# The last expert of a mixture-of-experts layer taken in the order of the others: its gate weights loaded ahead of the down weights of the expert before it, and its idle products removed

## The chip, the cores and the metric

The kernel runs on one core of a Trainium2 chip. The time is the device time of one execution in microseconds (us); several executions are timed, and their median counts. TensorE multiplies matrices, VectorE and ScalarE do elementwise work, SyncE (SP) issues the loads, which 16 transfer engines carry out. TensorE's clock has two levels, 1.2 and 2.4 GHz; the profile gives the granted clock as a share of the higher one.

## What is computed

One decoder layer for 256 tokens of width 1024: two attention branches, then 32 experts of which each token uses four, then a gated per-layer embedding (PLE). The change lies in the experts:

```python
def expert_block(args):
    xb, e = args
    gu = xb @ w_gate_up[e] + b_gate_up[e]
    g, u = gu[:, :D_EXPERT], gu[:, D_EXPERT:]
    g = jnp.minimum(g, SWIGLU_LIMIT)
    u = jnp.clip(u, -SWIGLU_LIMIT, SWIGLU_LIMIT)
    glu = g * jax.nn.sigmoid(SWIGLU_ALPHA * g)
    return ((u + 1.0) * glu) @ w_down[e] + b_down[e]
```

The rows of each expert are weighted and summed by token (`segment_sum`). Behind the experts comes `x + sigmoid(rmsnorm(x) @ w_ple_gate) * (p @ w_ple_proj)`.

## The kernel before

Every expert takes up to 64 tokens at once (an overflow loop handles more, and is not entered here). Its weights are float32: gate and up weights of 8 MiB in four tiles of 2 MiB, g0 to g3, and down weights of 4 MiB in two tiles, d0 and d1. Below, g31 stands for the gate and up weights of expert 31 or their products, d30 for the down weights of expert 30 or their products, and so on.

**Loads.** All weights stream through ten slots of 2 MiB in SBUF, in the order of the list `seq` (lines 138 to 147). `release` (line 150) is called when a tile has been used: it gives that slot to the next tile of the list, so a tile's load waits for the products that used the tile ten places earlier. SyncE issues the loads in that order at line 80; eight semaphore lanes are used in turn, so a load also waits until the load eight places earlier has landed. Only the last expert's tiles are loaded in two transfers of 1 MiB each. In the list, expert e's g tiles are followed by the d tiles of expert e-1; for the last expert (31) this is turned round: d30, then g31, then d31. Behind d31 come the two tiles of the PLE gate weights (w_ple, eight transfers of 0.5 MiB), then names that take a freed slot without a load: `low`, `hi`, `lo`, for the split halves of PLE operands.

**Products.** The loop over the experts is near line 945. `gate_up_k` (line 818) multiplies the gathered tokens xg with one k step of the gate and up weights, into the PSUM tiles g and u; a k step is four instructions of two passes each, an expert's eight k steps are 64 passes. `gate_up_bias` (line 812) adds the bias; `swiglu` (lines 822 to 828) is VectorE and ScalarE work; `hidden_T` (lines 834, 836) transposes the result on TensorE into PSUM and copies it on ScalarE to the tile ht. `down` runs 16 instructions of two passes (`down_k`, line 842) into the PSUM tile y and then `keep_y`: one half of y is copied to ys by ScalarE (line 846), the other by VectorE (line 847). Two experts share one ys; after each second expert `scatter` (line 852) adds both to the accumulators acc with eight passes. y, ht and ys have one buffer each.

In the loop, expert e's gate and up come first, then `down` of expert e-1, then the transposes of expert e: a down product fills the time of the swiglu. For the last expert `down` of 30 comes first; `keep_warm(WARM4, psum("y"))` issues 40 idle products (zeros, bfloat16, line 272) behind the bias. The instruction order on each engine is set by the tile framework's scheduler, which moved those 40 in among the gate products. Behind the loop come `down` of 31, ten idle products (WARM5), which the scheduler puts ahead of the transposes of 31, and the last scatter. Then acc is added to xs (line 999), xs is transposed (line 1004), and the PLE product runs with each operand split into a rounded part and a rest (w_hi, line 941, ScalarE; w_lo, line 942, VectorE; products at lines 251 to 253).

Of the kernel before, what the change touches and what calls it, by code (L numbers as in the profile page):

```python
# [33 lines left out]
NE = 32  # L34
# [20 lines left out]
FIRST_O = len(UNITS) - 8  # L55
LAST_THREE = 27

WARM0, WARM2, WARM3, WARM4, WARM5 = 30, 30, 8, 40, 10
AHEAD = 3

PLE_E, OVER_E = 14, 20
# [4 lines left out]
def hybrid_layer(ctx, tc, x, p, b_down, w_ple_gate, w_ple_proj, bgu3, xt, tabs, wpre, wgu, wdn, out):  # L66
# [59 lines left out]
    def bank(name):  # L126
        return ps_pool.tile([P, 512], F32, tag="ps", name=name)
# [12 lines left out]
    seq = []  # L140
    for e in range(NE):
        g = [(f"g{c}", e) for c in range(4)]
        d = [(f"d{c}", e - 1) for c in range(2) if e]
        seq += d + g if e == NE - 1 else g + d
        if e == PLE_E - 2:
            seq += [("aux", 0), ("pp", 0)]
        if e == OVER_E:
            seq += [("spare", 0), ("spare", 1)]
# [3 lines left out]
    def release(*slots):  # L152

        for i in slots:
            i = place.get(i, i)
            if sent[0] >= len(seq):
                return
            kind, e = seq[sent[0]]
            place[(kind, e)] = i
            t = v = slot(i, f"w_{kind}{e}")  # L160
            sent[0] += 1
            if kind[0] in "gd" and kind[1].isdigit():
                src = (wgu if kind[0] == "g" else wdn)[e, int(kind[1])]
                v = t.rearrange("p (k f) -> p k f", k=2 if kind[0] == "g" else 4)
                st = 2048 if e == NE - 1 else 4096
                for j in range(0, 4096, st):
                    load(t[:, j:j + st], src[:, j:j + st])
            elif kind == "aux":
                load(t[0:NE, 0:1024], b_down[0])
                load(t[:, 1024:1536].rearrange("p (t c) -> p t c", t=2), p[0, 0].rearrange("(t p) c -> t p c", p=P)  # L170
                     .rearrange("t p c -> p t c"))
                load(t[:, 2048:4096].rearrange("p (k f) -> p k f", k=2), w_ple_proj[0].rearrange("(k p) f -> p k f", p=P))
            elif kind == "ple":
                v = t.rearrange("p (k f) -> p k f", k=4)
                for k in range(4):
                    load(v[:, k], wpg[:, 4 * e + k])
            stream[(kind, e)] = v
# [90 lines left out]
    def keep_warm(n, b=None):  # L268

        b = bank("warm") if b is None else b  # L270
        for _ in range(n):
            T.matmul(b[:, 0:256], warm[:, 0:P], warm, start=True, stop=True)  # L272
# [441 lines left out]
    def work(tag, shape, bufs=1):  # L714
        return held[tag] if held else mo.tile(shape, F32, tag=tag, name=tag, bufs=bufs)
# [51 lines left out]
    def gather_pair(e):  # L767

        oh = work("oh", [P, 2, 2 * CAP])
        for tt in range(2):  # L770
            V.tensor_tensor(oh[:, tt].rearrange("p (j c) -> p j c", j=2), iota.rearrange("p (j c) -> p j c", j=2),
                            posm[:, tt, e:e + 2].unsqueeze(2).broadcast_to([P, 2, CAP]), op=ALU.is_equal)
        xg = work("xg", [P, 8, 2 * CAP])
        for half in range(2):
            b = psum("gu"[half])
            ks = slice(half * 4, half * 4 + 4)
            for k in range(4):
                for tt in range(2):
                    T.matmul(b[:, k * P:(k + 1) * P], h_perm[:, tt, (half * 4 + k) * P:(half * 4 + k + 1) * P],  # L779
                             oh[:, tt], start=(tt == 0), stop=(tt == 1))  # L780
            V.tensor_tensor(xg[:, ks], b.rearrange("p (k c) -> p k c", k=4),
                            gpk[:, 1, ks].unsqueeze(2).broadcast_to([P, 4, 2 * CAP]), op=ALU.mult)
        return xg, oh
# [3 lines left out]
    def weigh(ow, oh, wv_, odd):  # L787
        for tt in range(2):
            o = ow[:, tt].rearrange("p (g c) -> p g c", g=4)
            o = o[:, 1:3] if odd else o[:, 0:4:3]  # L790
            V.tensor_scalar(o, oh[:, tt:tt + 1].broadcast_to([P, 2, CAP]), wv_(tt), None, op0=ALU.mult)

    def weigh_pair(e, oh):
        ow = work("ow", [P, 2, S])
        for j in range(2):
            weigh(ow, oh[:, :, j * CAP:(j + 1) * CAP], wv_of(e + j), j)
        return ow
# [10 lines left out]
    def gate_up_bias(gu, se):  # L808
        for i in range(2):
            for half in range(2):  # L810
                w = bgu[:, i * 1024:(i + 1) * 1024].rearrange("e (q k) -> e q k", k=8)[:, :, half * 4:half * 4 + 4]
                T.matmul(gu[i][half * CAP:(half + 1) * CAP], se, w, start=False, stop=True)  # L812

    def gate_up_k(gu, xg, k, w):
        for i in range(2):
            for half in range(2):
                wv_ = w[:, i * 1024:(i + 1) * 1024].rearrange("p (q k) -> p q k", k=8)[:, :, half * 4:half * 4 + 4]
                T.matmul(gu[i][half * CAP:(half + 1) * CAP], xg[:, k], wv_, start=(k == 0), stop=False)  # L818

    def swiglu(gu):  # L820
        g = work("g", [P, 512])
        V.tensor_scalar_min(g, gu[0], 7.0)  # L822
        th = work("th", [P, 512])
        A.activation(th, g, AF.Tanh, scale=0.851)  # L824
        u = work("u", [P, 512])
        V.tensor_scalar(u, gu[1], 7.0, -7.0, op0=ALU.min, op1=ALU.max)
        V.scalar_tensor_tensor(u, in0=u, scalar=1.0, in1=g, op0=ALU.add, op1=ALU.mult)
        V.scalar_tensor_tensor(u, in0=th, scalar=1.0, in1=u, op0=ALU.add, op1=ALU.mult)
        return u

    def hidden_T(u):
        b = shared("hT")
        for j in range(4):
            T.transpose(b[:, j * P:(j + 1) * P], u.rearrange("p (q j) -> p q j", j=4)[:, :, j], ident)  # L834
        ht = work("ht", [P, 4, P])
        A.copy(ht, b.rearrange("p (j c) -> p j c", j=4))
        return ht

    def down_k(y, ht, f, w, odd):
        for dh in range(2):  # L840
            g = dh ^ odd
            T.matmul(y[g * CAP:(g + 1) * CAP], ht[:, f % 4, (f // 4) * CAP:(f // 4 + 1) * CAP],  # L842
                     w[:, dh * 512:(dh + 1) * 512], start=(f == 0), stop=(f == 7))

    def keep_y(ys, y, odd):
        A.copy(ys[0:CAP, odd], y[0:CAP])  # L846
        V.tensor_copy(ys[CAP:P, 1 - odd], y[CAP:P])  # L847
# [6 lines left out]
    def psum(tag):  # L854
        return held["ps_" + tag] if held else mps.tile([P, 512], F32, tag=tag, name=tag)
# [4 lines left out]
    def wv_of(e):  # L860
        return lambda tt: whalf[:, tt, e:e + 1]
# [65 lines left out]
    def down(e, ht, ys):  # L927
        y = psum("y")
        for f in range(8):
            down_k(y, ht, f, stream[(f"d{f // 4}", e)][:, f % 4], e % 2)  # L930
            if f % 4 == 3:
                release((f"d{f // 4}", e))
        keep_y(ys, y, e % 2)
# [10 lines left out]
    xg2, oh2 = gather_pair(0)  # L944
    weights()
    ow = weigh_pair(0, oh2)
    ht = None
    for e in range(NE):
        last, odd = e == NE - 1, e % 2
        if odd:  # L950
            ys = work("ys", [P, 2, 512])
        if last:
            down(e - 1, ht, ys)
        gu = [psum("g"), psum("u")]
        xg = xg2[:, :, odd * CAP:(odd + 1) * CAP]
        for k in range(8):
            gate_up_k(gu, xg, k, stream[(f"g{k // 2}", e)][:, k % 2])
            if k % 2:
                release((f"g{k // 2}", e))
        gate_up_bias(gu, id96[:, e:e + 1].broadcast_to([96, CAP]))  # L960
        u = swiglu(gu)
        if last:
            keep_warm(WARM4, psum("y"))
        else:
            if e:
                down(e - 1, ht, ys)
            if odd:
                xg2, oh2 = gather_pair(e + 1)
                ow = weigh_pair(e + 1, oh2)
        ht = hidden_T(u)  # L970
        if not odd:
            if e:
                scatter(ys, owT, first=(e == 2))
            owT = combine_T(ow)
        if e == OVER_E - 1:
            cnt = count()
        if e == OVER_E:
            overflow([stream[("spare", c)] for c in range(2)])
            release(("spare", 0), ("spare", 1))
        if e == PLE_E:  # L980
            aux = stream[("aux", 0)]
            pp = stream[("pp", 0)][:, 0:2048].rearrange("p (t c) -> p t c", t=2)
            down_bias()
            ple_projection()
            release(("aux", 0))
# [133 lines left out]
```

## Time and profile before

| | us |
|---|---|
| median of 3 timed runs | 1173.63 (1173.23 to 1173.77) |
| the profiled execution's own time | 1168.79 |
| its span, first to last instruction | 1167.0 |
| TensorE busy | 1083.0 (93%) |
| VectorE busy | 337.7 (29%) |
| ScalarE busy | 201.6 (17%) |
| transfer engines, share of the span taken by the weight queue q1 | 90.2% |
| mean granted clock of TensorE | 0.992 |

Busy times of TensorE are those of pipelined instructions with modelled ends: 16 passes of a down half lie 3.43 us long on the engine where the sum of their durations is far more. So durations of TensorE work are read from start to start. In the order of time a row has start, length, engine, line, operation, output<-inputs, shapes and count; the bracket gives the idle time ahead of it and what ended it. The chain of waits has start, length and what the end waited for there.

### The profile page before, as it was taken

How to read it: one execution, taken by the hardware profiler on the slowest of the kernel's cores; microseconds unless marked ns; L12 is line 12 of the kernel's file. 1: busy time of each engine (PE TensorE's matmuls, PEld its weight loads, DVE VectorE, ACT ScalarE, POOL GpSimd, SP SyncE). 2: the span in 40 equal slices, each digit the busy share in tenths (PEclk: the TensorE clock that was granted, in tenths of full speed). 3: DMA queues.
4: the chain of work that ended last, by engine and by line, in shares of the span. 5: the costliest groups of instructions: out<-in, count | busy, mean ns of one | idle time of the engine just before them, and what ended most of it. 6: DMA issues, size and time to landing. Idle time of an engine off the chain costs nothing. (4 is left out here: it accounts for less than half of the span.)

```text
span 1167.0 us, 13186 instructions
## 1 busy us (share of the span) xinstructions
PE 1083.0 (93%) x5486; PEld 529.2 (45%) x5486; DVE 337.7 (29%) x754; ACT 201.6 (17%) x375; POOL 78.5 (7%) x84
## 2 busy tenths in 40 slices
PE   8879999999999999998889999998899999998988
PEld 6668997543434343342333434333333333333336
DVE  7987686321111121121110111210111111111126
ACT  6557643210000000000001000000000000000024
POOL 6553320000000000000000000000000000000000
PEclk9999999999999999999999999999999999999999
DMA  9653568799999999999999999999899999999981
GB/s 368 223 177 108 200 209 323 288 430 430 431 430 431 430 429 430 431 431 411 431 431 431 431 430 430 431 430 426 349 430 430 431 430 431 431 430 430 425 352 37
DMA packets 39650, 440.19 MB, mean 377 GB/s; under 512 B 4384, under 2 KB 5152, under 8 KB 14144
## 3 DMA queue, kind: packets, MB, share of 16 engines
q1 hardware_dynamic: 39584, 439.27, 90.2%
q8 instruction: 46, 0.75, 0.2%
q14 instruction: 20, 0.16, 0.0%
HBM read 438.21 MB, written 1.05 MB: 376 GB/s over the span
## 5 line engine op out<-in xcount | busy, mean ns | idle before, releaser
L818 PE MATMUL g<-w_g,xg 128*64 128x512 f32 x1024 | 291.3, 599 | 26.7 <-DMA w_g<-in_wgu 22.2
L818 PE MATMUL u<-w_g,xg 128*64 128x512 f32 x1024 | 288.4, 595 | 0.0
L842 PE MATMUL y<-w_d,ht 128*64 128x512 f32 x1024 | 234.5, 596 | 12.5 <-DMA w_d<-in_wdn 11.7
L822 DVE TENSOR_SCALAR g<-g 128x512 f32<-128x512 f32 x32 | 22.1, 691 | 469.0 <-PE g L812 469.0
L818 PEld LDWEIGHTS g<-w_g,xg 128*64 128x64 f32 x1024 | 77.4, 137 | 169.1 <-issue 119.8
L818 PEld LDWEIGHTS u<-w_g,xg 128*64 128x64 f32 x1024 | 81.4, 137 | 145.5 <-issue 142.2
L842 PEld LDWEIGHTS y<-w_d,ht 128*64 128x64 f32 x1024 | 72.1, 136 | 137.2 <-issue 121.2
L824 ACT ACTIVATE th<-g 128x512 f32<-128x512 f32 x32 | 20.2, 630 | 487.9 <-DVE g L822 487.9
L847 DVE COPY ys<-y 64x512 f32<-64x512 f32 x32 | 22.2, 695 | 176.0 <-ACT ys L846 176.0
L852 PE MATMUL acc<-ys,owT 128*128 128x512 f32 x128 | 59.2, 605 | 9.5 <-ACT ys L846 9.5
L846 ACT COPY ys<-y 64x512 f32<-64x512 f32 x32 | 18.5, 578 | 262.0 <-PE y L842 262.0
L852 PEld LDWEIGHTS acc<-ys,owT 128*128 128x128 f32 x128 | 23.0, 189 | 46.5 <-ACT ys L846 21.8
L779 PE MATMUL g<-oh,h_perm 128*128 128x128 f32 x256 | 33.1, 282 | 6.8 <-DVE g L822 5.6
L210 ACT CAST fr<-raw_x 128x1024 fp32r<-128x1024 f32 (+1 forms) x33 | 33.9, 1033 | 22.5 <-PE proj L253 5.9
L779 PEld LDWEIGHTS g<-oh,h_perm 128*128 128x128 f32 x256 | 29.9, 191 | 16.9 <-DVE g L822 10.6
L214 POOL TENSOR_TENSOR fr<-raw_x,fr 128x384 fp32r<-128x384 f32 (+1 forms) x25 | 34.3, 1375 | 44.8 <-ACT fr L210 37.7
L214 DVE TENSOR_TENSOR fr<-raw_x,fr 128x640 fp32r<-128x640 f32 (+2 forms) x33 | 33.0, 999 | 6.2 <-ACT fr L210 6.0
L779 PEld LDWEIGHTS u<-oh,h_perm 128*128 128x128 f32 x256 | 29.8, 192 | 8.1 <-issue 8.1
L779 PE MATMUL u<-oh,h_perm 128*128 128x128 f32 x256 | 32.2, 279 | 0.0
L252 PE MATMUL proj<-fr,fr 128*128 128x512 f32 (+1 forms) x64 | 25.8, 403 | 6.9 <-DVE fr L214 6.2
L251 PE MATMUL gate<-fr,fr 128*128 128x256 f32 x104 | 31.2, 300 | 0.0
L253 PE MATMUL gate<-fr,fr 128*128 128x256 f32 x104 | 30.1, 290 | 0.0
(317 smaller groups left out, 1133.4 us busy)
## 6 DMA issues: line engine op xcount, KB each, us to landing
w_g<-in_wgu SPq DMA_DIRECT2D x124, 2048.0 KB, 31.1
w_d<-in_wdn SPq DMA_DIRECT2D x62, 2048.0 KB, 33.5
raw_x<-in_wpre SPq DMA_DIRECT2D x38, 512.0 KB, 4.2
w_g<-in_wgu SPq DMA_DIRECT2D x8, 1024.0 KB, 28.1
raw<-in_wpre SPq DMA_DIRECT2D x8, 512.0 KB, 6.6
w_d<-in_wdn SPq DMA_DIRECT2D x4, 1024.0 KB, 19.7
w_ple<-in_w_ple_gate SPq DMA_DIRECT2D x8, 512.0 KB, 14.5
raw<-in_wpre SPq DMA_DIRECT2D x4, 416.0 KB, 7.2
```

The lines of the kernel that those rows point to most:

```text
L210: A.copy(hi, src)
L214: e.tensor_tensor(lo[:, a:b], src[:, a:b], hi[:, a:b], op=ALU.subtract)
L251: T.matmul(o, lh, rh, start=first, stop=False)
L252: T.matmul(o, lh, rl, start=False, stop=False)
L253: T.matmul(o, ll, rh, start=False, stop=last)
L779: T.matmul(b[:, k * P:(k + 1) * P], h_perm[:, tt, (half * 4 + k) * P:(half * 4 + k + 1) * P], oh[:, tt], start=(tt == 0), stop=(tt == 1))
L818: T.matmul(gu[i][half * CAP:(half + 1) * CAP], xg[:, k], wv_, start=(k == 0), stop=False)
L822: V.tensor_scalar_min(g, gu[0], 7.0)
L824: A.activation(th, g, AF.Tanh, scale=0.851)
L842: T.matmul(y[g * CAP:(g + 1) * CAP], ht[:, f % 4, (f // 4) * CAP:(f // 4 + 1) * CAP], w[:, dh * 512:(dh + 1) * 512], start=(f == 0), stop= ...
L847: V.tensor_copy(ys[CAP:P, 1 - odd], y[CAP:P])
L852: T.matmul(acc[tt][dh], owT[:, dh, tok(tt)], ys[:, dh], start=first, stop=last)
```

## The change

It takes away three special cases of the last expert: the turned order in the list of loads, `down` of expert 30 ahead of the gate products of 31, and the 40 idle products. `down` of 30 now stands behind swiglu of 31, as for every other expert.

```diff
-WARM0, WARM2, WARM3, WARM4, WARM5 = 30, 30, 8, 40, 10
+WARM0, WARM2, WARM3, WARM5 = 30, 30, 8, 10
@@
         d = [(f"d{c}", e - 1) for c in range(2) if e]
-        seq += d + g if e == NE - 1 else g + d
+        seq += g + d
@@
         last, odd = e == NE - 1, e % 2
         if odd:
             ys = work("ys", [P, 2, 512])
-        if last:
-            down(e - 1, ht, ys)
         gu = [psum("g"), psum("u")]
@@
         u = swiglu(gu)
-        if last:
-            keep_warm(WARM4, psum("y"))
-        else:
-            if e:
-                down(e - 1, ht, ys)
-            if odd:
-                xg2, oh2 = gather_pair(e + 1)
-                ow = weigh_pair(e + 1, oh2)
+        if e:
+            down(e - 1, ht, ys)
+        if odd and not last:
+            xg2, oh2 = gather_pair(e + 1)
+            ow = weigh_pair(e + 1, oh2)
         ht = hidden_T(u)
```

How instructions move is shown at three places; the semaphores that an instruction waits for stand in brackets (DMAHW is a lane of the loads, Activation is ScalarE, DVE VectorE). In w_g031 the digits are tile 0 of expert 31.

SyncE, the loads of the last two experts, before:

```order
L80 DMA w_d129_5729<-in_wdn 128x4096 [waits DMAHW6_49,PE_49]
L80 DMA w_d030_5739<-in_wdn 128x4096 [waits DMAHW7_49,PE_49]
L80 DMA w_d130_5762<-in_wdn 128x4096 [waits DMAHW0_49,PE_49]
L80 DMA w_g031_5772<-in_wgu 128x2048 [waits DMAHW1_49,PE_49]
L80 DMA w_g031_5772<-in_wgu 128x2048 [waits DMAHW2_49]
```

and after:

```order
L80 DMA w_d129_5729<-in_wdn 128x4096 [waits DMAHW6_49,PE_49]
L80 DMA w_g031_5739<-in_wgu 128x2048 [waits DMAHW7_49,PE_49]
...
L80 DMA w_g331_5825<-in_wgu 128x2048 [waits DMAHW6_49]
L80 DMA w_d030_5836<-in_wdn 128x4096 [waits DMAHW7_49,PE_49]
L80 DMA w_d130_5846<-in_wdn 128x4096 [waits DMAHW0_49,PE_49]
L80 DMA w_d031_5856<-in_wdn 128x2048 [waits DMAHW1_49,PE_49]
```

The two loads of d30 moved behind the eight of g31; d31 and the w_ple loads behind it keep their places and lanes.

TensorE, from the second down half of expert 29 on, after (before, the sixteen instructions of d30 stood behind the transposes of ow at line 804, with g31 and the 40 idle products behind them):

```order
L842 MATMUL y_5871<-w_d129_5729,ht_5813 64x512 x7
L818 MATMUL g_5917<-w_g031_5739,xg_5782 64x512 [waits DMAHW7_49,PE_49]
L852 MATMUL acc_2250<-ys_5698,owT_5691 128x512 [waits Activation_49]
L852 MATMUL acc_2249<-ys_5698,owT_5691 128x512 [waits DVE_49]
L852 MATMUL acc_2251<-ys_5698,owT_5691 128x512
L852 MATMUL acc_2252<-ys_5698,owT_5691 128x512
L804 MATMUL owT_5910<-cst_62,ow_5803 128x128 [waits PE_49,Activation_49]
L804 MATMUL owT_5910<-cst_62,ow_5803 128x128 x3
L818 MATMUL g_5917<-w_g031_5739,xg_5782 64x512
```

One instruction (two passes) of g31 moved ahead of the scatter, and g31 follows owT directly. Further down, TensorE's end of the experts, after:

```order
L834 MATMUL hT_5992<-cst_62,u_5967 128x128 x3
L842 MATMUL y_5971<-w_d030_5836,ht_5903 64x512 [waits DMAHW7_49]
L842 MATMUL y_5971<-w_d030_5836,ht_5903 64x512 x7
L842 MATMUL y_5971<-w_d130_5846,ht_5903 64x512 [waits DMAHW0_49]
L842 MATMUL y_5971<-w_d130_5846,ht_5903 64x512 x7
L842 MATMUL y_5999<-w_d031_5856,ht_5997 64x512 [waits DMAHW1_49,DVE_49,Activation_49]
...
L852 MATMUL acc_2250<-ys_5916,owT_5909 128x512 [waits Activation_49]
L852 MATMUL acc_2252<-ys_5916,owT_5909 128x512
L852 MATMUL acc_2249<-ys_5916,owT_5909 128x512 [waits DVE_49]
```

d30 now lies between the transposes and d31, and the first product of d31 waits for VectorE and ScalarE, where before it waited for ScalarE alone.

ScalarE there, after:

```order
L824 ACTIVATE th_5965<-g_5963 128x512 [waits DVE_49,Activation_49]
L846 COPY ys_5916<-y_5971 64x512 [waits PE_49,Activation_49]
L836 COPY ht_5997<-hT_5992 128x512 [waits Activation_49]
L941 ACTIVATE w_hi0_5949<-w_ple0_5891,cst_62 128x1024 [waits DMAHW4_49,DMAHW5_49,DMAHW3_49,DMAHW6_49,DMAHW2_49,DMAHW7_49,DMAHW1_49,DMAHW0_49]
L846 COPY ys_5916<-y_5999 64x512 [waits PE_49]
```

The copy of expert 30's ys moved from ahead of line 824 to between it and the copy of ht; the first w_hi (line 941) stands ahead of the last copy of ys, and did before.

## Rows read from the trace of the kernel before

**Rows 1.** The page, transfer queues: packets, MB, share of 16 engines.

```profile
q1 hardware_dynamic: 39584, 439.27, 90.2%
```

**Rows 2.** Chain of waits from 1030 us on: start, length, what.

```profile
1046.23 39.91 DMA w_d<-in_wdn
1086.18 3.68 PE y L842 x16
```

**Rows 3.** TensorE in order of time, two windows (1056 and 1086 us on).

```profile
1058.34 0.64 PE L834 MATMUL hT<-cst,u 128*128 128x128 f32 x4
1058.91 3.65 PE L842 MATMUL y<-w_d,ht 128*64 128x512 f32 x16
...
1086.18 3.65 PE L842 MATMUL y<-w_d,ht 128*64 128x512 f32 x16 [0.42 <-DMA w_d<-in_wdn]
1090.52 3.70 PE L852 MATMUL acc<-ys,owT 128*128 128x512 f32 x8 [0.68 <-ACT ys L846]
...
1094.58 7.09 PE L842 MATMUL y<-w_d,ht 128*64 128x512 f32 x32
1101.50 1.03 PE L818 MATMUL g<-w_g,xg 128*64 128x512 f32 x4
...
1103.32 1.16 PE L272 MATMUL y<-warm 128*128 128x256 bf16 x9
...
1115.48 1.03 PE L818 MATMUL g<-w_g,xg 128*64 128x512 f32 x4
...
1119.77 1.03 PE L818 MATMUL u<-w_g,xg 128*64 128x512 f32 x4
1120.63 0.40 PE L812 MATMUL g<-bgu,id 96*64 96x512 bf16 x2
...
1123.93 0.75 PE L834 MATMUL hT<-cst,u 128*128 128x128 f32 x4 [0.87 <-DVE u L828]
1125.41 7.09 PE L842 MATMUL y<-w_d,ht 128*64 128x512 f32 x32 [0.73 <-ACT ht L836]
1133.17 1.12 PE L852 MATMUL acc<-ys,owT 128*128 128x512 f32 x2 [0.68 <-ACT ys L846]
```

**Rows 4.** SyncE's loads in order of time; then the w_ple tile's issues.

```profile
1098.37 7.79 SPq L80 DMA_DIRECT2D w_d<-in_wdn  x4
1108.36 17.38 SPq L80 DMA_DIRECT2D w_ple<-in_w_ple_gate  x8
...
L80 SPq DMA_DIRECT2D w_ple<-in_w_ple_gate x8: 327/328/328, 1108.4 to 1125.4; - x8
```

**Rows 5.** ScalarE (ACT), then VectorE (DVE), in order of time.

```profile
1089.88 0.58 ACT L846 COPY ys<-y 64x512 f32<-64x512 f32 x1 [8.05 <-PE y L842]
...
1126.92 1.15 ACT L941 ACTIVATE w_hi<-w_ple,cst 128x1024 fp32r<-128x1024 f32 x1 [1.57 <-DMA w_ple<-in_w_ple_gate]
1132.54 0.58 ACT L846 COPY ys<-y 64x512 f32<-64x512 f32 x1 [4.47 <-PE y L842]
1133.02 3.22 ACT L941 ACTIVATE w_hi<-w_ple,cst 128x1024 fp32r<-128x1024 f32 x3
...
1090.49 0.69 DVE L847 COPY ys<-y 64x512 f32<-64x512 f32 x1 [7.27 <-ACT ys L846]
1128.10 1.28 DVE L942 SCALAR_TENSOR_TENSOR w_lo<-w_ple,cst,w_hi 128x1024 fp32r<-128x1024 f32 x1 [4.23 <-ACT w_hi L941]
```

**Rows 6.** TensorE at 800.68; stretches: length, busy times, granted clock, transfer share, GB/s.

```profile
800.68 1.59 PE L818 MATMUL g<-w_g,xg 128*64 128x512 f32 x4 [3.96 <-PEq L898]
...
801.00:804.60 3.60, 3.60 (x12) 1.25 (x10) 0.00 (x0) 0.00 (x0) 0.00 (x0) 0.53 1.02 423
804.60:810.00 5.40, 5.40 (x28) 2.19 (x26) 0.00 (x0) 0.00 (x0) 0.00 (x0) 1.00 1.02 434
1120.60:1125.41 4.81, 2.65 (x21) 1.65 (x17) 2.67 (x4) 1.22 (x2) 0.00 (x0) 1.00 1.01 420
```

## The prediction

> **What bounds the kernel now.** I read the page first, then the chain of waits, then the order of time of each engine behind the point where the chain leaves the transfers. The weight queue q1 fills 90.2% of the transfer engines over the whole span [rows 1], and up to 1086.18 us the chain consists of landings: its last link there is a 39.91 us transfer of down weights [rows 2]. At 1086.18 TensorE starts the second half of expert 29's down product, released by that landing; behind it TensorE's rows name copies and VectorE as releasers, and no transfer [rows 3]. So the change, which touches nothing ahead of that point, has to be judged in the last 80 us, where the chain runs over TensorE: scatter, both down halves of expert 30 (1094.58), gate and up of expert 31 (1101.50 to 1120.63), bias, transposes (1123.93), down of 31 (1125.41), then the copies and the scatter.
>
> Two prices come from there. Six entries of gate/up, 1115.48 to 1120.63, take 5.15 us: 0.858 us an entry of 4 passes, 0.2146 us a pass, 13.73 us for an expert's 64 passes, 3.43 us for a down half of 16 [rows 3]. The stretch 1101.50 to 1120.63 is 19.13 us long, so the 40 idle products in it cost 5.40 us, on the path and not beside it.
>
> **The stream after the change.** The same bytes go out in the same place: 4 MiB of d30 ahead of 8 MiB of gate weights before, behind them now. Each load waits on the lane of the load eight earlier (the brackets of the listed order), so an issue time shows that one's landing: the first load of d31 went out at 1098.37, when the first 1 MiB piece of g31 had landed, the first ple load at 1108.36, when its fifth piece had [rows 4]. Counted from d29's landing at about 1086.15, that is 5 MiB in 12.2 us and 9 MiB in 22.2 us: 2.45 us per MiB, an estimate from these rows. The last of the eight ple loads went out at 1125.4, when the last piece of d31 had landed [rows 4]; 16 MiB by 2.453 from 1086.15 gives the same. So after the change: g31's eight pieces land at 1088.6, 1091.1 ... 1105.8; d30's halves at 1110.7 and 1115.6; d31's four pieces at 1118.0, 1120.5, 1122.9 and 1125.4, as before; the first ple piece unchanged. These loads also wait for their slots. The first ple load is a close one: it goes out when g31's seventh piece has landed, at about 1103.3, and its slot is freed by the first half of d29, which lies ahead of 1086.18: 17 us of cover. So I cost the queue at nothing; if that cover were gone, a late load would eat the slack of step 6 first and then count in full.
>
> **TensorE after the change, step by step.**
> 1. At 1089.61 (1086.18 plus 3.43) it has 0.91 us to wait for the copy of ys, since the scatter starts at 1090.52 [rows 3, 5]. Two passes of g31 now stand ahead of the scatter and fit there: 0.43 us gained. Their piece landed at 1088.6.
> 2. Scatter and owT end at 1094.58 as before. Then 62 passes of g31: 13.31 us, to 1107.89. Each of the eight k steps starts after its piece; the closest is the last, 1106.2 against 1105.8. The 5.40 us of idle products are gone.
> 3. Bias, clamps, ten idle products and transposes follow at the old distance, 1120.63 to 1123.93: transposes at 1111.19. The next down half follows transposes that nothing holds up after 0.57 us (1058.34 to 1058.91) [rows 3]: d30 starts at 1111.76, its weights landed at 1110.7. Before, d31 had to wait 1.48 us there for the copy of ht: 0.91 us gained.
> 4. The second half of d30 is wanted at 1115.19 and lands at 1115.6: 0.4 us lost. End 1119.06.
> 5. A new wait: y and ht have one buffer each. ys of expert 30 must leave y, and ht of 31 can be written only when d30 has read the old ht; both copies stand in that order on ScalarE, and VectorE copies its half of ys after ScalarE's. The same pattern after 1089.61 takes 0.27 us to ScalarE's copy, 0.58 for it, then 0.69 on VectorE, to 1091.18 [rows 5], and about 0.05 to the waiting product (there the scatter starts 0.06 us after ScalarE's copy ends). So d31 starts 1.62 us after 1119.06, at 1120.68: 1.62 us lost; no product is left to fill it. Queued behind it are d31 and the tail.
> 6. d31's 32 passes take 6.87 us, to 1127.55; its pieces are wanted at 1120.68, 1122.4, 1124.1 and 1125.83 and land at 1118.0, 1120.5, 1122.9 and 1125.4. Slack at the last: 0.4 us. Before, the end was 1132.28. Sum for TensorE: -5.40 - 0.43 - 0.91 + 0.4 + 1.62 = -4.7 us.
> 7. The first w_hi stands ahead of the last ys copy on ScalarE. In the trace it runs from 1126.92, released by its transfer, for 1.15 us, and is hidden by d31 [rows 5]. The cover shrinks: the copy could start 0.26 us after d31, as before (1132.28 to 1132.54), at 1127.81; it starts when the w_hi has ended, at 1128.0 to 1128.1. 0.2 us lost. The first w_lo (1128.10, 1.28 us) also delays VectorE's copy, to 1130.0, but only the third scatter product needs that one, 1.7 us after the first.
>
> By the Trainium skill (TensorE: Matmul & The Clock Gate, section on the array's architectural detail, queue depths) ScalarE and VectorE are strictly first in, first out, which speaks against the change in step 7: work that is ready waits behind the w_hi. No row of the trace shows a ready copy held. By the rule the sum is -4.5; if the copy could pass the w_hi it would be -4.7.
>
> The scatter starts 0.63 us after the start of that copy, as before: about 4.5 us earlier (1133.17 to 1128.6). The tail's VectorE and ScalarE work hangs on it, and the ple pieces are there in time: w_hi 2 to 4 follow each other every 1.07 us (3.22 for three [rows 5]), from 1128.5 on; at the stream's rate a 0.5 MiB piece comes every 1.2 us, the second at 1127.9 and the fourth at 1130.3, wanted at 1130.6. By the same rate the eighth lands by 1135.3, before the second four w_hi, which stand behind the transposes, begin. So the tail moves whole. 1168.79 - 4.5 = 1164.3 us for a profiled execution; that execution was 4.84 us under the median of the runs, 1173.63, so for the median **1169.1 us**.
>
> Bounds: the gain can't pass 5.2 us (last piece of d31 at 1125.4, its four passes and more 1.72 us, end 1127.1). From below: step 5 bounded by twice its row, step 4 by a piece that comes a whole piece (2.45 us) later, give a gain of 4.5 - 1.6 - 2.1 = 0.8 us if both happened; either alone leaves 2.4 to 2.9.
>
> **Rivals.**
> - *A clock dip, then a smaller gain.* Without idle products TensorE stands 1.62 us (step 5) and 1.1 us (ahead of the scatter) right behind d30 and d31. Against it: between 1120.60 and 1125.41 it worked only 2.65 us of 4.81, in pieces, and the granted clock stayed 1.00. For it: after one wait of 3.96 us the clock of the following 3.6 us averaged 0.53, half of 2.4 GHz [rows 6]. One such dip loses 3.6 x 0.47 = 1.7 us: gain 2.8, 1170.8 us. Chance 0.10. The Trainium skill (the same page, HAM oscillation) warns of exactly this, a TensorE that waits between bursts and starts each again slow; the trace agrees at that one wait, and doesn't at the shorter ones between 1120.60 and 1125.41.
> - *Slower: the clock at half through the whole end.* d30, d31, scatter and the ple products are now packed between short waits; if each wait brought a dip, the loss is half the time at 1.2 GHz. It decides at 9 us of half clock (4.5 us lost). Half clock from 1111.8 to 1127.5 doubles 64 passes: 13.7 us lost, 1178.3 us. Behind the wait of 3.96 us the clock was back at 1.00 from 804.60 on [rows 6], so a dip didn't last. Chance 0.03.
> - *The stream is the new bound, little gain.* If the pieces of d30 or d31 come late, TensorE waits for them with all 64 down passes still to do, where before 32 of them were done early. A stream 3.5 us late at d30's second half gives a loss of 3.9 in place of 0.4, 1172.6 us: no change that can be told. For it: all slack is 0.4 us. Against: same bytes, same lanes, 2.45 us per MiB on both checks. Chance 0.06, and 0.05 more for a lag of 1 to 2 us, 1170.1 to 1171.1.
> - *The change doesn't do what it says*, and the loads keep their order: the listed order shows them moved. No change in time; chance 0.01.
>
> **Numbers.** Forecast 1169.1 us, chance 0.75. Range 1167.6 (a gain of 6.0: the bound of 5.2 and 0.8 for two medians of runs that spread by 0.54 us) to 1171.2 (dip, or the short lag). About 0.2%, 2.35 us here, is what a measurement can tell from no change: faster by more 0.90, within it 0.07, slower 0.03.
>
> **What would show it.** In the new profile: TensorE's gate/up of 31 unbroken from 1094.6 to 1107.9 with no transfer named; d30 at about 1111.8; an idle of 1.6 us before d31 put down to a ys or ht copy; scatter near 1128.6 right behind a ScalarE queue of w_hi and ys; granted clock 1.00 throughout. Wrong would be: transfer waits above 0.5 us inside g31, a clock under 1.00 after 1111, or the tail's first ple product waiting on w_hi or w_lo.

## The result and the profile after

The changed kernel took 1166.79 us (median of 4 runs, 1165.23 to 1167.72), the kernel before beside it 1173.7 us (4 runs, 1173.23 to 1174.87): 0.9942 of the time, 95% interval 0.9928 to 0.9956, a gain of 6.9 us. The forecast was 1169.1 us in a range of 1167.6 to 1171.2, a gain of 4.5 us: the direction is right, the time lies 0.8 us below the range.

| | before | after |
|---|---|---|
| the profiled execution's own time, us | 1168.79 | 1165.23 |
| its span, us | 1167.0 | 1163.5 |
| q1's share of the span | 90.2% | 90.7% |
| second half of d29 to the last scatter, us | 46.99 | 42.62 |
| last scatter to the end of the span, us | 33.83 | 33.9 |

The fourth row is the length of the stretch that the change touches, from the last product that a transfer releases to the scatter: 1086.18 to 1133.17 in [rows 3], and 1086.98 to 1129.60 here. It is 4.37 us shorter. The chain of waits shows the same layout: the last landing, then TensorE to the end of the experts (start, length, what ended there).

```profile
1046.94 40.00 DMA w_d<-in_wdn
1086.98 3.65 PE y L842 x16
...
1121.84 7.10 PE y L842 x32
1128.97 0.59 ACT ys L846
1129.60 2.00 PE acc L852 x4
```

TensorE of the changed kernel in order of time, columns as in [rows 3]:

```profile
1086.98 3.65 PE L842 MATMUL y<-w_d,ht 128*64 128x512 f32 x16 [0.43 <-DMA w_d<-in_wdn]
1090.47 1.02 PE L818 MATMUL g<-w_g,xg 128*64 128x512 f32 x2
1091.42 3.70 PE L852 MATMUL acc<-ys,owT 128*128 128x512 f32 x8
...
1095.49 0.64 PE L818 MATMUL g<-w_g,xg 128*64 128x512 f32 x1
...
1108.46 0.40 PE L812 MATMUL g<-bgu,id 96*64 96x512 bf16 x1
1108.69 0.39 PE L812 MATMUL u<-bgu,id 96*64 96x512 bf16 x1
1108.85 0.59 PE L818 MATMUL u<-w_g,xg 128*64 128x512 f32 x1
1109.28 0.39 PE L812 MATMUL g<-bgu,id 96*64 96x512 bf16 x1
1109.51 0.39 PE L812 MATMUL u<-bgu,id 96*64 96x512 bf16 x1
1110.45 1.25 PE L272 MATMUL g<-warm 128*128 128x256 bf16 x10 [0.56 <-DVE g L822]
1112.57 0.75 PE L834 MATMUL hT<-cst,u 128*128 128x128 f32 x4 [0.87 <-DVE u L828]
1113.25 7.09 PE L842 MATMUL y<-w_d,ht 128*64 128x512 f32 x32
1121.84 7.09 PE L842 MATMUL y<-w_d,ht 128*64 128x512 f32 x32 [1.51 <-ACT ht L836]
1129.60 3.70 PE L852 MATMUL acc<-ys,owT 128*128 128x512 f32 x8 [0.67 <-ACT ys L846]
```

Two passes of g31 stand ahead of the scatter; g31 runs unbroken; d30 has taken the place of d31 behind the transposes, without the 0.73 us wait for ht; d31 has the new wait of 1.51 us. No row behind 1086.98 names a transfer. ScalarE's rows for the end, then VectorE's copy of the other half of expert 30's ys:

```profile
1120.43 0.58 ACT L846 COPY ys<-y 64x512 f32<-64x512 f32 x1 [9.31 <-PE y L842]
1120.92 0.58 ACT L836 COPY ht<-hT 128x512 f32<-128x512 f32 x1
1127.63 1.15 ACT L941 ACTIVATE w_hi<-w_ple,cst 128x1024 fp32r<-128x1024 f32 x1 [6.13 <-DMA w_ple<-in_w_ple_gate]
1128.97 0.58 ACT L846 COPY ys<-y 64x512 f32<-64x512 f32 x1 [0.19 <-PE y L842]
...
1121.05 0.69 DVE L847 COPY ys<-y 64x512 f32<-64x512 f32 x1 [8.53 <-ACT ys L846]
```

The first w_hi ends at 1128.78; the copy behind it waits 0.19 us more, for TensorE, so w_hi held nothing. SyncE's rows give the stream (start and length of a group of issues):

```profile
1089.47 12.50 SPq L80 DMA_DIRECT2D w_d<-in_wdn  x6
1104.13 22.36 SPq L80 DMA_DIRECT2D w_ple<-in_w_ple_gate  x8
```

The first w_ple load goes out at 1104.13 (forecast: 1103.3, and this execution stands 0.80 us later), the last at 1126.49 (1104.13 and 22.36; forecast 1125.4, and 0.80). The stream ran as worked out, to 0.3 us.

So one question is left: the profile shows 4.4 us, the first runs 6.9.

### The profile page after: what moved, and what is told of

It is laid out like the page before. It is cut to its first block, busy times and chain, and to the rows that moved or that the text cites. A ratio compares the mean times of both kernels' runs of the same rounds, so it can differ in the third digit from the quotient of the medians.

```text
span 1163.5 us, 13110 instructions
## 1 busy us (share of the span) xinstructions
PE 1076.0 (92%) x5446; PEld 525.8 (45%) x5446; DVE 337.9 (29%) x754; ACT 201.4 (17%) x375; POOL 78.2 (7%) x84
## 3 DMA queue, kind: packets, MB, share of 16 engines
q1 hardware_dynamic: 39584, 439.27, 90.7%
HBM read 438.21 MB, written 1.05 MB: 378 GB/s over the span
## 5 line engine op out<-in xcount | busy, mean ns | idle before, releaser
L818 PE MATMUL g<-w_g,xg 128*64 128x512 f32 x1024 | 295.4, 597 | 28.3 <-DMA w_g<-in_wgu 24.3
L818 PE MATMUL u<-w_g,xg 128*64 128x512 f32 x1024 | 292.5, 593 | 0.0
L210 ACT CAST fr<-raw_x 128x1024 fp32r<-128x1024 f32 (+1 forms) x33 | 33.9, 1033 | 21.8 <-PE proj L253 5.6
```

The lines of the kernel that those rows point to most:

```text
L210: A.copy(hi, src)
```

## The experiments

All distances run from the start of d29's second half. "Interval" ends at the last scatter, "end" at the end of the span. The runs come in groups ("calls" in the expectations), each on one chip; "beside" means the runs of the kernel before in the same group. The ratio is that of the kernel to the runs beside it, with its 95% interval; it is not exactly the ratio of the two medians.

**The two kernels again (b2, a2).** No edit.

> The kernel before, once more. The interval read in each profile here is the one from the start of d29's second half on TensorE to the start of the last scatter; it was 46.99 us before and 42.62 us after the change, 4.37 us less, where the medians of the runs differ by 6.9 us. Theory A: the change is worth its interval, 4.4 us; the other 2.5 us are chance between executions, lost far ahead of d29 (the granted clock was 0.96 in 600 to 640 us and in 780 to 820 us of the one profile of before, and 1.00 in that of after). Then this profile shows 47.0 us (within 0.3) whatever its span, and a span longer than 1167 comes with more stretches under 1.00 ahead of 1080 us. Theory B: the profile of before was an untypical execution, and in its timed runs the end itself is longer, by a clock under 1.00 or a transfer wait behind d29. Then a profile with a span near 1172 us shows an interval near 49.4 us.

> The changed kernel once more. Theory A: interval 42.6 us (within 0.3), time 4 to 5 us under the kernel before when enough runs of both are taken (ratio 0.996). Theory B: ratio 0.994 again (7 us), with this interval unchanged and that of before longer.

b2: 1171.89 us (12 runs, 1166.87 to 1175.67) and beside it 1171.58 (33 runs). a2: 1167.75 us (10 runs), ratio 0.9964 [0.9951, 0.9978], 3.8 us. The first base, 1173.2 to 1174.9, lay high in a spread of 8.8 us. The interval of a2 is 42.62 us, as in the first profile. That of b2 is 48.69 (from 1086.82), neither theory's figure, 47.0 or 49.4:

```profile
1124.57 0.75 PE L834 MATMUL hT<-cst,u 128*128 128x128 f32 x4 [0.87 <-DVE u L828]
1126.04 8.78 PE L842 MATMUL y<-w_d,ht 128*64 128x512 f32 x32 [0.73 <-ACT ht L836]
1135.51 3.70 PE L852 MATMUL acc<-ys,owT 128*128 128x512 f32 x8 [0.68 <-ACT ys L846]
```

d31 takes 8.78 us where it took 7.09 in [rows 3]: 1.69 us more, all of the difference. The windows around it (length, TensorE's busy time, granted clock, transfer share, GB/s) show why:

```profile
1120.00:1126.00 6.00, 3.89 (x26) 1.00 1.01 421
1126.00:1130.00 4.00, 3.96 (x12) 0.57 1.04 422
1130.00:1136.00 6.00, 5.32 (x25) 1.00 0.66 268
```

Over 4.00 us the granted clock was 0.57, which is 3.4 us at the lower of its levels (1.2 GHz), inside d31, behind the waits of 0.87 and 0.73 us; half of 3.4 us is the 1.7 lost.

**The idle products alone (e1, e2).** e1 is the kernel before without them, e2 the changed kernel with them.

```diff
 # e1, in the kernel before
-            keep_warm(WARM4, psum("y"))
+            pass
@@
 # e2, in the changed kernel, behind swiglu
+        if last:
+            keep_warm(40, psum("y"))
```

> The kernel before without the 40 idle products, loads and down products in the old order. By the step list: g31 would run from 1101.5 without the 5.40 us, but its pieces land at 1098.4 + 2.45 j, so from the fifth k step on it waits for transfers; the last piece lands at 1115.5, g31 ends at 1117.3 in place of 1120.6: interval 46.99 - 3.3 = 43.7 us, time 3.3 us less than before. If the idle products alone made the whole gain (order of no use): interval 42.6. If their place were free time: 47.0.

> The changed kernel with the 40 idle products back (the scheduler puts them among the last k steps of g31). The step list: g31 5.3 us longer, the wait for d30's second half (0.4 us) gone: interval 42.6 + 4.9 = 47.5 us, time within 1 us of the kernel before. If the new order of loads and products gave a gain of its own of several us: interval under 46 us.

e1: 1168.28 us (12 runs), ratio 0.9968 [0.9955, 0.9981]; interval 43.62. Without the idle products the last three k steps of g31 wait for their pieces (0.38, 0.48 and 0.50 us), since d30's bytes still come first. The start of the interval, one of the three rows, and the end:

```profile
1090.82 3.65 PE L842 MATMUL y<-w_d,ht 128*64 128x512 f32 x16 [0.42 <-DMA w_d<-in_wdn]
...
1120.12 1.08 PE L818 MATMUL g<-w_g,xg 128*64 128x512 f32 x4 [0.50 <-DMA w_g<-in_wgu]
...
1126.67 7.09 PE L842 MATMUL y<-w_d,ht 128*64 128x512 f32 x32 [0.73 <-ACT ht L836]
1134.44 3.70 PE L852 MATMUL acc<-ys,owT 128*128 128x512 f32 x8 [0.68 <-ACT ys L846]
```

46.99 less 43.62 is 3.37 us for taking the idle products out alone. e2: 1171.57 us (12 runs), ratio 1.0 [0.9987, 1.0014]; interval 48.02, 5.40 more than the changed kernel and 0.5 more than expected (0.4 of it is the wait for d30's second half, which the expectation took off and which the changed kernel doesn't have):

```profile
1089.66 3.65 PE L842 MATMUL y<-w_d,ht 128*64 128x512 f32 x16 [0.44 <-DMA w_d<-in_wdn]
...
1137.68 3.70 PE L852 MATMUL acc<-ys,owT 128*128 128x512 f32 x8 [0.67 <-ACT ys L846]
```

With the new order of loads the idle products are paid in full; with the old one a part of them covered transfers. The intervals also show that the new order alone, with the idle products still in, is no gain: 48.02 against 46.99 is 1.03 us longer.

**The order of loads undone (e4)**, beside the changed kernel once more (a3).

```diff
-        seq += g + d
+        seq += d + g if e == NE - 1 else g + d
```

> The changed kernel once more, beside kernels of the same call. Theory A (what the change is worth is the shortening of TensorE's end, 4.37 us, and the 6.9 us of the first medians was drawn from executions that spread by 7 to 9 us): the difference of medians from the kernel before is 3.4 to 5.0 us, and from the second half of expert 29's down product to the scatter lie 42.6 us. Rival B (the kernel before loses a further 2.5 us in a typical execution that its first profile did not show): difference 6 to 7.5 us.

> The changed kernel with the order of loads undone: d30's weights before g31's again, no idle products, products listed as in the change. Theory A (the idle products are worth about 3.4 us net, the order of loads and products about 1.0 us): interval from expert 29's second half to the scatter 43.6 to 43.7 us, 1.0 more than the changed kernel, and a median 0.5 to 1.5 us above it. Rival B (order is worth nothing beside the idle products): interval 42.6, no difference.

a3: 1166.53 us (6 runs), ratio 0.9949 [0.9936, 0.9962], 5.5 us; interval 42.61. e4: 1169.4 us (10 runs), ratio 0.9975 [0.9965, 0.9985], 2.9 us above a3, more than forecast. Its profile has the old order of products (the scheduler puts d30 where its weights are) and the loss in d31 again:

```profile
1085.83 3.65 PE L842 MATMUL y<-w_d,ht 128*64 128x512 f32 x16 [0.42 <-DMA w_d<-in_wdn]
...
1121.67 8.78 PE L842 MATMUL y<-w_d,ht 128*64 128x512 f32 x32 [0.73 <-ACT ht L836]
1131.13 3.70 PE L852 MATMUL acc<-ys,owT 128*128 128x512 f32 x8 [0.68 <-ACT ys L846]
```

The interval is 45.30 us; without the 1.69 us in d31 it is 43.61, e1's length and the one expected. Without the idle products the order of loads and products is worth 1.0 us at full clock; rival B falls.

**The new wait taken away (x1), then w_hi behind the copy (x2).** x1 gives d31 another PSUM tile, which is free by then, and its ht a spare tile; x2 also lets the first w_hi read its scale from a copy that ScalarE makes behind the last copy of ys.

```diff
 # x1, in hidden_T (spare is set for expert 31) and down
-        ht = work("ht", [P, 4, P])
+        ht = work("ow", [P, 2, S]).rearrange("p a (b c) -> p (a b) c", b=2) if spare else work("ht", [P, 4, P])
@@
-        y = psum("y")
+        y = psum("u" if e == NE - 1 else "y")
@@
-        ht = hidden_T(u)
+        ht = hidden_T(u, last)
@@
 # x2 as well, in split_ple (line 942, for w_lo, takes the copied scale too)
+        if k == 0:
+            gp2[0] = work("ow", [P, 2, S])[:, 0, 0:8]
+            A.copy(gp2[0], gpk[:, 2])
@@
-        A.mul(wh[k], wg, gpk[:, 2, k:k + 1])
+        A.mul(wh[k], wg, gp2[0][:, k:k + 1])
```

> The changed kernel with d31 accumulated in a PSUM tile that is free by then, and its ht written to a spare tile, so that d31 no longer waits for the copies of ys and ht. Theory A (behind the new wait stands the first w_hi on ScalarE, which ends about 19.1 us after d30 starts ... at 1128.8 on the changed kernel's scale, and the last piece of d31, which lands at about 1126.1): d31 starts right behind d30, waits about 0.6 us for its last piece, ends at 1127.8, the copy of ys is held by w_hi to 1128.8: interval from expert 29's second half to the scatter 42.3 to 42.4 us, 0.2 to 0.3 less than the changed kernel. Rival B (the new wait of 1.51 us is worth its full length, nothing stands behind it): 41.1 us.

> The same, and the first w_hi placed behind the last copy of ys on ScalarE (its scale is copied by ScalarE behind d31, which makes it wait). Theory A (w_hi is what holds the copy once the wait is gone): copy of ys at about 1128.1 on the changed kernel's scale, interval to the scatter 41.7 to 41.8 us, 0.9 less than the changed kernel; the end of the span gains 0.3 to 0.9, since the first w_lo now follows the first addition to xs. Rival B (the transfer of d31's last piece sets the end of d31, not ScalarE's queue): interval 42.3 or more as without the second edit.

x1: 1166.11 us (6 runs), ratio 0.995 [0.9936, 0.9964], no different from a3. TensorE, then ScalarE, of x1:

```profile
1088.86 3.65 PE L842 MATMUL y<-w_d,ht 128*64 128x512 f32 x16 [0.44 <-DMA w_d<-in_wdn]
...
1122.04 3.60 PE L842 MATMUL u<-w_d,ow 128*64 128x512 f32 x16
1125.81 1.94 PE L842 MATMUL u<-w_d,ow 128*64 128x512 f32 x8 [0.17 <-DMA w_d<-in_wdn]
1128.25 1.94 PE L842 MATMUL u<-w_d,ow 128*64 128x512 f32 x8 [0.50 <-DMA w_d<-in_wdn]
1131.37 3.70 PE L852 MATMUL acc<-ys,owT 128*128 128x512 f32 x8 [1.18 <-ACT ys L846]
```

```profile
1129.70 1.15 ACT L941 ACTIVATE w_hi<-w_ple,cst 128x1024 fp32r<-128x1024 f32 x1 [6.81 <-DMA w_ple<-in_w_ple_gate]
1130.76 0.56 ACT L846 COPY ys<-u 64x512 f32<-64x512 f32 x1
```

d31 starts right behind d30 and then waits for its last two pieces, 0.67 us in all; the copy of ys follows w_hi without a gap, and the scatter waits 1.18 us in place of 0.67. (In the changed kernel w_hi ends 15.5 us behind the start of d30; the 19.1 us of the expectation is a slip, its 1128.8 is right.) Of 1.51 us taken away 0.11 are left: interval 42.51 (forecast 42.3 to 42.4). Rival B, 41.1, falls. x2 moves w_hi out of the way: 1166.66 us (6 runs), ratio 0.9945 [0.9928, 0.9962], interval 41.82 as forecast, with the ends of the interval and ScalarE's rows

```profile
1089.40 3.65 PE L842 MATMUL y<-w_d,ht 128*64 128x512 f32 x16 [0.42 <-DMA w_d<-in_wdn]
1131.22 3.70 PE L852 MATMUL acc<-ys,owT 128*128 128x512 f32 x8 [0.68 <-ACT ys L846]
...
1130.59 0.58 ACT L846 COPY ys<-u 64x512 f32<-64x512 f32 x1 [7.15 <-PE u L842]
...
1131.30 3.23 ACT L946 ACTIVATE w_hi<-w_ple,ow 128x1024 fp32r<-128x1024 f32 x3
```

and an end at 75.3 us, 1.2 less than a3's. The times don't show it; it was run again below.

**How often does d31 lose clock (b3, b4), and does the wait for ht do it (e5)?** e5 is the kernel before with the transposes of expert 31 done twice, the second time into a free PSUM tile, so that TensorE works during the copy of ht.

```diff
+        for j in range(4 if fill is not None else 0):
+            T.transpose(fill[:, j * P:(j + 1) * P], u.rearrange("p (q j) -> p q j", j=4)[:, :, j], ident)
@@
-        ht = hidden_T(u)
+        ht = hidden_T(u, psum("u") if last else None)
```

> One more profile of the kernel before, to see how often an execution loses clock in the last down product. So far d31 took 7.09 us in two of four profiles with the old order of products and 8.78 us, at a granted clock of 0.50 for three microseconds, in the two others; d30 and d31 took 7.09 us in all six profiles with the new order. Theory C (with the old order the 0.73 us wait for ht stands behind the waits of the swiglu, and in part of the executions the clock falls there): d31 8.78 us with a chance of one half. Theory D (the two were accidents that strike either order alike): 7.09 us with a chance of four fifths.

> The same again. Theory C: d31 8.78 us with a chance of one half; theory D: 7.09 us with a chance of four fifths.

> The kernel before with the four transposes of expert 31 done a second time, into a free PSUM tile, right behind the first: 0.55 us of work laid into the 0.73 us in which TensorE waits for the copy of ht; nothing it computes changes. Theory C (that wait is what tips the clock over): d31 takes 7.09 us, and the interval from expert 29's second half to the scatter stays 47.0 us, since the added work lies under the wait. Theory D: 8.78 us with a chance of one fifth.

> The same kernel once more, as one profile can't tell a chance of one half from none. Theory C: again 7.09 us and 47.0 us. Theory D: 8.78 us with a chance of one fifth.

b3 and b4 show d31 at 8.78 us, intervals 48.69 and 48.68, and took 1171.07 and 1171.19 us (one run each). The two runs of e5 took 1170.33 and 1173.83 us; both profiles show 7.09 us and an interval of 46.99, the first from 1087.63:

```profile
1125.38 0.75 PE L834 MATMUL hT<-cst,u 128*128 128x128 f32 x4 [0.87 <-DVE u L828]
1125.96 0.65 PE L836 MATMUL u<-cst,u 128*128 128x128 f32 x4
1126.85 7.09 PE L844 MATMUL y<-w_d,ht 128*64 128x512 f32 x32 [0.25 <-ACT ht L838]
1134.62 3.70 PE L854 MATMUL acc<-ys,owT 128*128 128x512 f32 x8 [0.68 <-ACT ys L848]
```

That is what theory C expects, and theory D doesn't exclude it: it gives each of the two profiles four chances in five of the same. The next runs test theory C by times, and the other way round.

**e5 timed; the wait put into the new order (e6); the changed kernel (a4) and x2 beside them.** e6 has x1's spare tile for ht, emits the transposes of 31 ahead of d30 and lets d30 accumulate in their PSUM tile, so that d30 waits for the copy of ht.

```diff
# in down
-        y = psum("y")
+        y = shared("y") if e == NE - 2 else psum("y")
@@
-        if e:
+        if last:
+            ht, ht30 = hidden_T(u, True), ht
+            down(e - 1, ht30, ys)
+        elif e:
             down(e - 1, ht, ys)
```

> The kernel before with the wait for ht ahead of d31 filled by repeated transposes, now timed, and a third profile. Theory C (the wait tips the clock in about two of three executions, 1.7 us each): 0.8 to 1.5 us faster than the kernel before in the mean, d31 7.09 us. Theory D (accidents): no difference, d31 8.78 us possible.

> The changed kernel with d30 accumulated in the PSUM tile of the transposes, so that d30 must wait for the copy of ht of expert 31 (0.73 us), just as d31 did in the kernel before; ht of 31 goes to a spare tile and d31 no longer waits. Theory C: d30 takes 8.78 us in place of 7.09 us with a chance of two thirds; interval to the scatter 42.4 to 42.6 us without the loss, about 43.2 us with it. Theory D: d30 7.09 us with a chance of four fifths or more.

> The changed kernel beside them. Both theories: d30 and d31 7.09 us, interval 42.6 us. Theory C: 4.4 us plus 0.8 to 1.5 us, 5.2 to 5.9 us in all, below the kernel before; theory D: 4.4 us below.

> The version without the wait ahead of d31 and with the first w_hi behind the copy of ys, once more. Its first profile ended 75.3 us behind expert 29's second half, the changed kernel's 76.4 to 76.5 us. Theory A (the 1.1 us is real): 0.7 to 1.5 us under the changed kernel of the same call, though the spread may hide it. Rival: no difference, the clock takes it back elsewhere.

e5: 1170.96 us (12 runs), ratio 1.0004 [0.9988, 1.0019]; d31 7.09 us in the third profile too. The times decide nothing: the median is 0.8 us under the 1171.78 of the 28 runs beside it, the ratio shows no gain, and a gain of 1.0 us (0.9991) lies inside its interval. e6: 1166.69 us (10 runs), ratio 0.9955 [0.9939, 0.9972]; the wait is there, the loss isn't, and the interval is 42.31, near the 42.4 to 42.6 expected without it:

```profile
1116.83 7.09 PE L842 MATMUL y<-w_d,ht 128*64 128x512 f32 x32 [0.68 <-ACT ow L836]
1123.75 7.20 PE L842 MATMUL y<-w_d,ow 128*64 128x512 f32 x32
1132.13 3.70 PE L852 MATMUL acc<-ys,owT 128*128 128x512 f32 x8 [1.18 <-ACT ys L846]
```

So theory C isn't settled: nothing in e6 speaks for it, and one profile without the loss doesn't exclude a chance of two thirds. a4: 1166.0 us (8 runs), ratio 0.9954 [0.9935, 0.9972], 5.8 us by the medians; interval 42.62. x2: 1166.56 us (11 runs), ratio 0.9957 [0.9941, 0.9973], its end at 75.2 us, so the profile's 1.2 us are there a second time and the times again don't tell it from a4. The intervals are 2 us wide to either side; x2 is no faster than the changed kernel as far as these runs can tell.

**The two kernels on one more chip (b5, a5).**

> The kernel before once more. Theory A (executions spread, the first runs lay high in the spread): median 1171 to 1172.5 us, like the runs of the other calls. Rival B (the first medians were typical of some chips): 1173 us or more. Theory C: d31 8.78 us with a chance of two thirds.

> The changed kernel beside it. Theory A: median 1166 to 1167.5 us, 4.4 to 5.5 us below the kernel before, d30 and d31 7.09 us, interval 42.6 us. Rival B: 6 us or more below.

b5: 1172.0 us (12 runs), and beside it 1171.64 (17 runs); its profile has d31 at 7.09 us and an interval of 47.0. a5: 1165.76 us (6 runs), ratio 0.9939 [0.9924, 0.9955], 5.9 us; interval 42.62, d30 and d31 7.09 us. The base is theory A's, the gain of this group is just above its 5.5 us. Theory C had given 8.78 us two chances in three here.

**All groups together.** The kernel before: 124 runs, median 1171.66 us, 1166.87 to 1175.67. The changed one: 34 runs, median 1166.74, 1162.53 to 1169.79. The difference of the medians is 4.9 us (95%: 3.9 to 6.2, by drawing the runs again); by group it was 6.9, 3.8, 5.5, 5.8 and 5.9. The spread goes with the granted clock of the whole execution: of the kernel before, 9 runs at a mean of 0.994 took 1170.33 us on average, 21 runs at 0.988 took 1172.89. Of the 120 later runs of the kernel before, 23 reached 1173.23, the lowest of the first four.

## Why the prediction missed, step by step

Times from d29's second half, predicted and found:

| step | predicted | found |
|---|---|---|
| scatter of 29, behind two passes of g31 (1) | 4.34 | 4.44 |
| g31 starts again (2) | 8.40 | 8.51 |
| transposes of 31 (3) | 25.01 | 25.59 |
| d30 (3) | 25.58 | 26.27 |
| wait inside d30 (4) | 0.4 | none |
| d31 (5) | 34.50 | 34.86 |
| last scatter (7) | 42.42 | 42.62 |

**The mechanism was right**, and nearly its sum: 4.5 us forecast to the scatter, 4.37 found. Single steps were off by more. d30 came 0.69 us late, and most of that didn't reach the scatter, since it took up the two waits that were forecast behind it, 0.4 us in d30 and 0.2 us behind w_hi.
- *Steps 1 and 2* held to 0.1 us. The idle products went for their full price (e2 against the changed kernel: 5.40).
- *Step 3* was 0.6 us short. I let the bias follow "at the old distance". In [rows 3] and the row below, which follows there, its four products stand in pairs, x2, 0.23 us from pair to pair; in the changed kernel the halves of g and u alternate, with a g31 product among them. From the first bias product to the last it is 1.05 us (1108.46 to 1109.51), 0.43 of it for the g31 product, where it was 0.23: 0.4 us more. g31 itself took 0.1 us more, and d30 followed the transposes after 0.68 us where 0.57 was forecast.

```profile
1120.86 0.39 PE L812 MATMUL u<-bgu,id 96*64 96x512 bf16 x2
```

- *Step 4*: no wait. d30's start, 0.69 us later than forecast, used up the 0.4 us.
- *Step 5*: the new wait is there. Its bracket names the copy of ht, which ends at 1121.50; but VectorE's copy of ys, the one that the forecast took for the last, ends later, at 1121.74, 0.10 us ahead of d31. No run separates the two. From d30's start to d31's it is 8.59 us, 1.72 more than the 6.87 of the products, forecast 1.62.
- *Step 6*: no transfer wait in d31. x1 shows how near the pieces are: with d31 1.7 us earlier it waits 0.67 us for the last two of them.
- *Step 7*: w_hi held nothing, 0.2 us not lost, since d31 ended later than forecast. x1 shows the mechanism once d31 ends earlier: a ready copy stands behind w_hi for 0.5 us (d31's end, 1128.25 and 1.72, and the usual 0.26 make 1130.23; it starts at 1130.76, and the scatter waits 0.5 us more), and with w_hi behind it, in x2, it starts 0.26 us after the end of d31. There the strict order that the Trainium skill states (TensorE: Matmul & The Clock Gate, section on the array's architectural detail) is seen in a row of this kernel.
- *The whole tail moved*, as forecast: 33.83 us before, 33.9 after.

**The step that failed is the last one, from the profiled execution to the median**: "that execution was 4.84 us under the median of the runs, 1173.63, so for the median 1169.1 us". It took three runs within 0.54 us for the kernel's median, and the same 0.54 us for the spread in the range's low end. Over 124 runs the median is 1171.66, 2.0 us lower, and the spread is 8.8 us. From that base the same sum gives 1167.2 us, in agreement with 1166.79 and with 1166.74 over 34 runs. 2.0 of the 2.3 us of error are thus the base; the rest (4.9 against 4.5) lies inside the interval. Why the first four runs lay so high stays open. Plain chance is a poor account of it: 23 of 120 later runs reached their lowest, so four such runs in a row have a chance of about one in 700 (an estimate from that share). The changed kernel's runs of the same group, 1166.79, agree with its 30 later ones, 1166.56.

**What the offset held.** An offset may be added only if both kernels have it. The profiles show a part that the two may not share: b3 took 2.3 us longer than the profiled execution of [rows 3], 1.7 of it inside d31. Every profile with the old order of products and nothing in the wait for ht: d31 at 8.78 us in 4 of 7 (b2, b3, b4, e4; not in the first one, b5 and e1). With the new order 8.78 us did not occur in 10 profiles, nor in e5's three. So the rival "a clock dip" had the size right, 1.7 us, and the kernel wrong: where a profile shows it, it belongs to the order before. That the wait for ht brings it is not shown: e6 has the same waits and no loss, in one profile. 4 in 7 of 1.7 us on top of 4.4 would make 5.3 us; 4.9 [3.9, 6.2] holds both. Whether this loss is a part of the timed gain stays open: taking it out of the kernel before (e5) moved no time that can be told.

The rival "slower by half clock" had no trace (granted clock 1.00 in d30 and d31); the stream was not the bound, though in x1, with d31 earlier, its last two pieces come 0.17 and 0.50 us too late; the change did what it says. One price of the rivals was summed wrongly: 13.7 us lost on a forecast of 1169.1 make 1182.8 us, not 1178.3.

## What to carry to other kernels

- A sum of steps read from one execution was good to 0.2 us here, where the steps lie behind the last wait for a transfer; the base it is taken from was off by 2.0. A few close runs don't bound the spread, and an execution 4.8 us under its median calls for the question which loss its profile lacks and whether the changed kernel would have it too.
- Taking one wait away at the end of a chain is worth the distance to the next one: 1.51 us gave 0.11 (x1), and 0.80 once the queue behind it was reordered as well (x2).
- Filler work on the path costs its length less what it covers: the same 40 products were worth 3.37 us with the old order of loads and 5.40 with the new one. And the new order was worth 1.0 us without them and cost 1.0 us with them, so two parts of a change are not priced one by one. Look also at which pairs of instructions a new order tears apart.

## What the runs showed of the hardware

- Executions of one kernel on one chip spread by 8.8 us (b2: 1166.87 to 1175.67). Over all groups those at a higher mean granted clock are the shorter ones (0.994: 1170.33 us on average, 0.988: 1172.89). The profiles differ ahead of the change too: d29's second half starts between 1085.83 (e4) and 1091.11 us (e5_again).
- A 32-pass down product took 8.78 us in place of 7.09 when the clock fell behind waits of 0.56, 0.87 and 0.73 us (b2: 0.57 granted over 4.00 us), in some executions and not in others with the same rows; at the 1.51 us wait ahead of d31 in the changed kernel it fell in none of five profiles. The Trainium skill (TensorE: Matmul & The Clock Gate, HAM oscillation) describes a TensorE that waits for transfers between bursts of products and starts each burst slow. The four profiles show such a slow start, but behind short waits for VectorE and ScalarE; the five show none, and no run here says which executions are struck.
- Two bias products that write the two halves of one tile take 0.23 us together when they stand next to each other (1120.63 to 1120.86 in the kernel before, x2). Where the halves of g and u alternate, one product takes as long (1108.46 to 1108.69 and 1109.28 to 1109.51 of the changed kernel).
